# Seven-product pairs at every second place of the last product, and four buffers for each split part, in a two-layer hybrid trunk

## The chip, the core and the metric

The kernel runs on one core of a Trainium2 chip. Its time is the device time of one execution in microseconds (us); of several runs the median is taken. Five engines work side by side, each through its own queue in a fixed order: TensorE (PE) multiplies, VectorE (DVE) and ScalarE (ACT) do elementwise work, GpSimd (POOL) and SyncE (SP) mostly issue DMA transfers. They wait for each other by semaphores.

## The reference

One layer over 256 tokens of width 2048, all in float32:

```
h  = rmsnorm(x, norm1_g);  z = h @ w_in
a_out = forgetting_attention(...);  m_out = rmsnorm(mlstm(...)) * sigmoid(o)
merged = sigmoid(g_a) * (a_out @ w_proj_a) + sigmoid(g_m) * (m_out @ w_proj_m)
x  = x + merged @ w_out
h2 = rmsnorm(x, norm2_g)
u  = causal_dwconv(h2 @ w_up, conv_w, conv_b)          # 2 x 5632 channels, 3 taps
x  = x + (silu(u_gate) * u_val) @ w_down               # 5632 x 2048
```

The last line is the last product. It is the place where most of the change lies.

## The kernel before

**Two parts for each number.** TensorE multiplies in a short format (fp32r), so each float32 operand is split into a high part, which ScalarE rounds, and a low part, which VectorE makes as the difference between the operand and its high part. A product then takes three matmuls: low part of the activations by high weights, high by high, and high by low. The weights arrive as tiles `raw` of 128x2048 (three buffers, loaded on SP's queue, line 132). `split_sub` cuts each tile into pieces and makes `wh` on ScalarE (line 169) and `wl` on VectorE (line 170) for each piece, 128x1024 as a rule. There are three buffers of `wh` and three of `wl`, in turn. `next_sub(ahead)` hands the next piece to the matmuls and splits up to `ahead` pieces, that one included: two in most stages, three in `s_block`.

**Stages.** In order: the columns of `w_in` (`mog`, `fq`, `fk`, `fv`, `mk`, `mq`, `mv`), the gates (`g0` to `g3`), the two projections (`p`), the product with `w_out` (`wo0`, `wo1`), the product with `w_up` (`up`, 88 blocks), and the last product in two halves of 1024 columns, `y0` and `y1`.

**The last product.** 5632 rows of `w_down` make 44 blocks of 128, taken two at a time: 22 pairs for each half. A pair is done in one of two ways, by a string with one letter a pair (`Y_PAIRS`). A plain pair (`p`) has two pieces and eight products: 24 matmuls with 512 columns. A seven-product pair (`S`) is a Strassen-like scheme with seven products, 21 matmuls, in four pieces named `b` (two products), `b21` (one product, 128x512), `t13` and `t24` (two products each). `t13` and `t24` are sums and differences of the weights, which VectorE makes in a tile `sums`: line 154 from `b`'s tile (128x1024), then lines 161 and 164 (128x512 each). So an S costs VectorE three more operations than its low parts, and its last two pieces depend on them. The S products go into four accumulators `y0p`/`y1p`, the others into `y0q`/`y1q`; after the last S of a half a chain of one ScalarE copy and eight VectorE additions (lines 339 and 298) adds the `p` accumulators into `xr`, two of them behind each piece that follows; the half ends with four additions of `q` (line 974) and four stores.

**The ring.** The S pairs also need sums of the activations. They are made while `up` runs (`put_sums`), written to a tile in DRAM (`s_dram`, line 937) and read back by POOL's queue into ring tiles `s_ops`, each for two S pairs (line 952). One function, `load_sums`, is called twice ahead of the last product and then once whenever a new ring tile begins to be used, so that three tiles are in use or on their way.

**Where the order comes from.** The code is recorded as it is written, and a scheduler puts the instructions of each engine in a fixed order, as it finds them ready by its own reckoning; earlier-written work goes first. `issue_after(x)` forbids it to put an instruction ahead of `x`. Before the change the first operation on `sums` (line 154) is held behind the last write of the `up` stage alone, in the last product; nothing holds it in the earlier stages, so the scheduler may draw it forward among low parts.

**Large tiles.** Activations, gates, `sums` and ring tiles share one set of 15 buffers of 8 KB a partition (`a8`). While `up` runs, four of them hold its input `h2` and eleven the result (`ghl`).

Of the kernel before, what the change touches and what calls it, by code (L numbers as in the profile page):

```python
# [1 line left out]

# [1 line left out]

# [6 lines left out]
F32 = mybir.dt.float32  # L11
F32R = mybir.dt.float32r
# [5 lines left out]
P = 128  # L18
# [17 lines left out]
PLAIN = "p" * 8  # L36
G_PAIRS = "pSpSpSpp"
WO_PAIRS = "pSpSpppp"
Y_PAIRS = "ppp" + "SSpSp" * 3 + "Sp" + "pp"
N_S = Y_PAIRS.count("S")  # L40


# [18 lines left out]
def trunk(ctx: ExitStack, tc: tile.TileContext, a):  # L61
# [14 lines left out]
        return psaux.tile([P, 512], F32, tag="aux", name=name)  # L76

    def a8(name, shape, dtype=F32):
        return big.tile([P, *shape], dtype, tag="a8", bufs=15, name=name)

    def scratch(name, shape, tag="w2k", bufs=4):
        return work.tile(shape, F32, tag=tag, bufs=bufs, name=name)
# [51 lines left out]
    def split_sub(j):  # L134
        if j >= len(subs_of) or j in subs:
            return
        i, s, kind = subs_of[j]
        load_chunk(i)
        if j < KD:
            put(hT[j][:, 0, :], hT[j][:, 1, :], xT[j], cst[:, C_G1 + j : C_G1 + j + 1])  # L140
        n = 512 if kind == "b21" else chunks[i][1] // 2
        raw, sums = raws[i], s_tiles.get("sums")


        if kind == "whole":
            src = raw[:, s * n : (s + 1) * n]
        elif kind == "b":
            src = raw[:, 512:1536]
            if s_tiles["of"] != chunks[i][2]:
                s_tiles["of"] = chunks[i][2]  # L150
                s_tiles["sums"] = a8(f"sums{i}", [2048])
            sums = s_tiles["sums"]
            with tc.issue_after(last_of["up"].ins) if "up" in last_of else nullcontext():
                nc.vector.tensor_tensor(  # L154
                    sums[:, :1024].rearrange("p (i c) -> p i c", i=2),
                    raw[:, :512].unsqueeze(1).to_broadcast([P, 2, 512]),
                    src.rearrange("p (i c) -> p i c", i=2), ALU.subtract,
                )
        elif kind == "b21":
            src = raw[:, 1536:]  # L160
            nc.vector.tensor_tensor(sums[:, 1024:1536], raw[:, 1024:1536], sums[:, :512], ALU.subtract)
        elif kind == "t13":
            src = sums[:, :1024]
            nc.vector.tensor_tensor(sums[:, 1536:], raw[:, 1536:], sums[:, 1024:1536], ALU.subtract)
        else:
            src = sums[:, 1024:]
        wh = wpool.tile([P, 1024], F32R, tag="wh", bufs=3, name=f"wh{j}")
        wl = wpool.tile([P, 1024], F32R, tag="wl", bufs=3, name=f"wl{j}")
        nc.scalar.activation(wh[:, :n], src, AF.Copy)  # L169
        nc.vector.tensor_tensor(wl[:, :n], src, wh[:, :n].bitcast(F32), ALU.subtract)  # L170
        subs[j] = (wh[:, :n], wl[:, :n])

    state = {"sub": 0}
# [1 line left out]
    def next_sub(ahead=2):  # L175
        j = state["sub"]
        state["sub"] = j + 1
        i = subs_of[j][0]
        for c in range(i, i + 3):
            load_chunk(c)  # L180
        for q in range(j, j + ahead):
            split_sub(q)
        return subs.pop(j)
# [93 lines left out]
    def s_block(name, pairs, s_ops, pattern, pools, dst, add=True, per_piece=0):  # L277


        q = [[pools[0](f"{name}q{tok}{h}") for h in range(2)] for tok in range(2)]  # L280
        ps, late, left = {}, [], pattern.count("S")
        n_s = left

        def prod(out, x, w, c, first, last):
            wh, wl = w[0][:, c * 512 : (c + 1) * 512], w[1][:, c * 512 : (c + 1) * 512]
            mm(out, x[1], wh, first, False)
            mm(out, x[0], wh, False, False)
            mm(out, x[0], wl, False, last)

        def piece():  # L290
            w = next_sub(3)
            for _ in range(min(2, len(late))):
                late.pop(0)()
            run_tasks(per_piece)
            return w

        def tt(o, x, y):
            late.append(lambda: nc.vector.tensor_tensor(o, x, y, ALU.add))

        for m, kind in enumerate(pattern):  # L300
            def op(i, tok):
                t = slice(tok * P, (tok + 1) * P)
                return pairs[m][:, i, 0, t], pairs[m][:, i, 1, t]

            if kind == "p":
                last = m == len(pattern) - 1
                ws = [piece(), piece()] if last else []

                todo = (
                    [(i, tok, h) for h in range(2) for tok in range(2) for i in range(2)] if last  # L310
                    else [(i, tok, h) for i in range(2) for h in range(2) for tok in range(2)]
                )
                for i, tok, h in todo:
                    if i == len(ws):
                        ws.append(piece())
                    prod(q[tok][h], op(i, tok), ws[i], 1 - h, m == 0 and i == 0, last and i == 1)
                continue
            first, last = left == n_s, left == 1
            left -= 1
            s1, s2, s3, s4 = s_ops[m]  # L320
            w = piece()
            if first:
                ps = {i: pools[1](f"{name}p{i}") for i in (1, 5, 7, 6)}
            prod(ps[1], op(0, 0), w, 0, first, last)
            prod(q[0][1], s4, w, 1, False, False)
            prod(q[0][0], op(1, 0), piece(), 0, False, False)
            w = piece()
            prod(ps[5], s1, w, 0, first, last)
            prod(ps[7], s3, w, 1, first, last)
            w = piece()  # L330
            prod(ps[6], s2, w, 0, first, last)
            prod(q[1][0], op(1, 1), w, 1, False, False)
            if not last:
                continue
            c11, c12, c21, c22 = (dst(tok, h) for tok in range(2) for h in range(2))
            u2 = scratch("u2", [P, 512])
            if add:
                u3 = scratch("u3", [P, 512])
                late.append(lambda: nc.scalar.activation(u2, ps[1], AF.Copy))
                tt(c11, c11, ps[1])  # L340
                tt(u2, u2, ps[6])
                tt(u3, u2, ps[7])
                tt(u2, u2, ps[5])
                tt(c21, c21, u3)
                tt(u3, u3, ps[5])
                tt(c12, c12, u2)
                tt(c22, c22, u3)
            else:
                late.append(lambda: nc.scalar.activation(c11, ps[1], AF.Copy))
                tt(u2, c11, ps[6])  # L350
                tt(c21, u2, ps[7])
                tt(c12, u2, ps[5])
                tt(c22, c21, ps[5])
        for f in late:
            f()
        return q
# [564 lines left out]
    for j in range(NF):  # L921
# [12 lines left out]
        if Y_PAIRS[m] == "S":  # L934
# [3 lines left out]
                s_dram[:, n_s * 6 * P : (n_s + 1) * 6 * P], se.rearrange("p l c -> p (l c)")  # L938
            )
            n_s += 1  # L940
        last_of["up"] = put_pair(g_pairs[m], gv)


    s_pos = [m for m, kind in enumerate(Y_PAIRS) if kind == "S"]
# [13 lines left out]
        at = [ring[r][:, q * P : (q + 1) * P] for q in range(6 * i, 6 * i + 6)]  # L958
        return [(g[:, 0, 0, P:], g[:, 0, 1, P:])] + [(at[c], at[3 + c]) for c in range(3)]

    for _ in range(2):
        load_sums()
    for b in range(2):
        pools = (acc_tile, aux_tile) if b == 0 else (aux_tile, acc_tile)
        xr = big.tile([P, 2, 1024], F32, tag="mv", name=f"xr{b}")
# [86 lines left out]
```

## Time and profile before

| | |
|---|---|
| median of 3 runs | 1402.15 us (1394.18 to 1404.11) |
| the profiled execution | 1393.67 us, span 1391.9 us |
| PE busy | 1375.6 us, 99% |
| DVE busy | 1070.9 us, 77% |
| ACT busy | 767.2 us, 55% |
| `up` begins / last product begins / its second half begins | 661.9 / 1150.7 / 1269.8 us |
| TensorE clock granted | 1.00 in all stages |
| weight tile of `w_down`, issue to landing | 4.9 us median |
| ring tile, issue to landing | 4.7 us median, 4.4 to 10.6 |

The span goes from the first to the last instruction of the profiled execution; its own time is 1.8 us longer than the span. Start times are counted from the span's start. A matmul with 512 columns is shown as 0.39 us long, but the next one starts about 0.227 us after it, since matmuls are pipelined: time lost on PE is seen as a longer step between starts, and only the larger part of it as idle time.

### The profile page before, as it was taken

The numbers are of one execution on the slowest core, as the hardware profiler recorded it, in microseconds if no ns is written. First come the engines' busy times: TensorE is split into PE (matmuls) and PEld (weight loads), VectorE is DVE, ScalarE is ACT, GpSimd is POOL, SyncE is SP. The second block draws the span as 40 slices with busy tenths as digits, with TensorE's granted clock in tenths as the row PEclk, the third lists the DMA queues.
The fourth block names the chain that finished last, engine by engine and source line by source line (L and its number), as shares of the span: only waits on it lengthen the run. The fifth ranks groups of instructions, "written<-read, shape, count | busy, mean of one in ns | idle before, by whom it ended". The sixth has DMA issues, their size and how long they took to land.

```text
span 1391.9 us, 18433 instructions
## 1 busy us (share of the span) xinstructions
PE 1375.6 (99%) x6940; PEld 1157.2 (83%) x6940; DVE 1070.9 (77%) x1524; ACT 767.2 (55%) x1096; POOL 40.4 (3%) x73
## 2 busy tenths in 40 slices
PE   9999999999999999999999999999999999999998
PEld 8878888887888888888888888888888887778776
DVE  5655766556888867777878888888878888887987
ACT  6645554444665544555655555555655655553553
POOL 2101000000000000000000000000000000000000
PEclk9999999999999999999999999999999999999999
DMA  8645454443554565555555655655555657668553
GB/s 312 229 165 184 179 209 155 152 151 134 196 215 182 214 241 194 190 220 203 191 186 194 218 193 190 222 186 196 201 212 194 230 196 266 226 251 291 205 209 119
DMA packets 44073, 281.76 MB, mean 202 GB/s; under 512 B 5008, under 2 KB 5024, under 8 KB 13264
## 3 DMA queue, kind: packets, MB, share of 16 engines
q1 hardware_dynamic: 39168, 260.20, 52.4%
q0 software_dynamic: 4672, 20.38, 4.2%
q8 instruction: 54, 0.88, 0.2%
q14 instruction: 35, 0.29, 0.1%
q10 hardware_dynamic: 144, 0.02, 0.0%
HBM read 272.45 MB, written 8.13 MB: 202 GB/s over the span
## 4 chain that ended last, share of the span: by engine, by line
PE 96%; DVE 1%; issue 1%; ACT 1%; DMA 1%; POOL 0%; DVEq 0%; ACTq 0%; POOLq 0%
PE up L230 35%; PE p L230 6%; PE y1q L230 6%; PE y0q L230 5%; PE mog L230 3%; PE fq L230 3%; PE mv L230 3%; PE fk L230 3%; PE fv L230 3%; PE wo0q L230 3%; PE wo1q L230 3%; PE g1q L230 2%; PE g3q L230 2%; PE g2q L230 2%; PE g0q L230 2%; PE y1p L230 2%
## 5 line engine op out<-in xcount | busy, mean ns | idle before, releaser
L169 ACT ACTIVATE wh<-raw 128x1024 fp32r<-128x1024 f32 (+2 forms) x496 | 502.7, 1017 | 473.9 <-PE up L230 117.9
L170 DVE TENSOR_TENSOR wl<-raw,wh 128x1024 fp32r<-128x1024 f32 (+2 forms) x496 | 575.1, 1169 | 205.3 <-ACT wh L169 203.5
L230 PE MATMUL up<-h,wh 128*128 128x512 f32 x1408 | 488.6, 394 | 0.0
L230 PE MATMUL up<-h,wl 128*128 128x256 f32 x1408 | 390.0, 277 | 0.0
L230 PEld LDWEIGHTS up<-h,wh 128*128 128x128 f32 x1408 | 263.9, 188 | 61.4 <-DVE h L199 0.2
L230 PEld LDWEIGHTS up<-h,wl 128*128 128x128 f32 x1408 | 264.4, 188 | 0.1
L170 DVE TENSOR_TENSOR wl<-sums,wh 128x1024 fp32r<-128x1024 f32 x66 | 80.6, 1222 | 43.9 <-ACT wh L169 43.5
L169 ACT ACTIVATE wh<-sums 128x1024 fp32r<-128x1024 f32 x66 | 69.9, 1060 | 78.6 <-PE y0q L230 16.6
L909 DVE SCALAR_TENSOR_TENSOR t<-u,cst,t 128x256 f32<-128x256 f32 x176 | 84.7, 481 | 3.8 <-ACT t L907 0.7
L230 PE MATMUL p<-wh,am 128*128 128x512 f32 x256 | 79.6, 392 | 0.0
L230 PE MATMUL y1q<-wh,ghl 128*128 128x512 f32 x232 | 71.7, 390 | 0.0
L230 PE MATMUL y0q<-wh,ghl 128*128 128x512 f32 x232 | 71.7, 390 | 0.0
L230 PEld LDWEIGHTS p<-wh,am 128*128 128x128 f32 x256 | 47.6, 188 | 9.7
L907 ACT ACTIVATE t<-u,cst 128x256 f32<-128x256 f32 x88 | 52.0, 591 | 2.4 <-DVE u L904 1.9
L230 PEld LDWEIGHTS y1q<-wh,ghl 128*128 128x128 f32 x232 | 43.6, 188 | 9.2
L230 PEld LDWEIGHTS y0q<-wh,ghl 128*128 128x128 f32 x232 | 43.5, 188 | 9.1
L230 PE MATMUL p<-wl,am 128*128 128x512 f32 x128 | 49.9, 390 | 0.0
L230 PE MATMUL y1q<-wl,ghl 128*128 128x512 f32 x116 | 44.8, 391 | 0.0
L230 PE MATMUL y0q<-wl,ghl 128*128 128x512 f32 x116 | 44.8, 390 | 0.0
L154 DVE TENSOR_TENSOR sums<-raw 128x1024 f32<-128x1024 f32 x33 | 40.4, 1223 | 4.7 <-DMA raw<-in_w_dn 3.0
L230 PE MATMUL mog<-wh,hT 128*128 128x348 f32 (+1 forms) x192 | 42.4, 331 | 1.3 <-ACT wh L169 1.3
L230 PE MATMUL g0q<-wh,hN 128*128 128x512 f32 x128 | 41.3, 401 | 0.0
(370 smaller groups left out, 2064.0 us busy)
## 6 DMA issues: line engine op xcount, KB each, us to landing
raw<-in_w_up SPq DMA_DIRECT2D x88, 1024.0 KB, 4.9
raw<-in_w_dn SPq DMA_DIRECT2D x44, 1024.0 KB, 4.9
raw<-in_w_g SPq DMA_DIRECT2D x32, 1024.0 KB, 4.9
raw<-in_w_fox SPq DMA_DIRECT2D x24, 1024.0 KB, 4.9
raw<-in_w_p SPq DMA_DIRECT2D x16, 1024.0 KB, 4.8
raw<-in_w_out SPq DMA_DIRECT2D x16, 1024.0 KB, 4.8
raw<-in_w_mqk SPq DMA_DIRECT2D x8, 1024.0 KB, 4.8
raw<-in_w_mv SPq DMA_DIRECT2D x8, 1024.0 KB, 4.8
```

The source lines that it names most:

```text
L154: nc.vector.tensor_tensor(sums[:, :1024].rearrange("p (i c) -> p i c", i=2), raw[:, :512].unsqueeze(1).to_broadcast([P, 2, 512]), src.rear ...
L169: nc.scalar.activation(wh[:, :n], src, AF.Copy)
L170: nc.vector.tensor_tensor(wl[:, :n], src, wh[:, :n].bitcast(F32), ALU.subtract)
L230: nc.tensor.matmul(out, lhsT, rhs, start=start, stop=stop)
L907: nc.scalar.activation(t, u[:, 2:], AF.Identity, scale=w[2], bias=w[3])
L909: nc.vector.scalar_tensor_tensor(out=t, in0=u[:, i : i + S], scalar=w[i], in1=t, op0=ALU.mult, op1=ALU.add)
```

## The change

`Y_PAIRS` goes from `pppSSpSpSSpSpSSpSpSppp` to `pSpSpSpSpSpSpSpSpSpSpp`: ten S pairs as before, but never two in a row, with the first at place 1 in the place of 3 and the last at place 19 in the place of 18. In `s_block` four pieces are split ahead in the place of three, and there are four buffers each of `wh` and `wl`. These two hold for the gates and `w_out` too, which use the same function. The memory for them comes from the large tiles: 14 in the place of 15. The ring is two tiles: `load_sums` is called once ahead, not twice. The first operation on `sums` is now held, in all stages, behind the low part that was recorded last.

```diff
-Y_PAIRS = "ppp" + "SSpSp" * 3 + "Sp" + "pp"
+Y_PAIRS = "p" + "Sp" * 10 + "p"
...
-        return big.tile([P, *shape], dtype, tag="a8", bufs=15, name=name)
+        return big.tile([P, *shape], dtype, tag="a8", bufs=14, name=name)
...
-            with tc.issue_after(last_of["up"].ins) if "up" in last_of else nullcontext():
+
+            with tc.issue_after(last_of["wl"].ins):
                 nc.vector.tensor_tensor(
                     sums[:, :1024].rearrange("p (i c) -> p i c", i=2),
...
-        wh = wpool.tile([P, 1024], F32R, tag="wh", bufs=3, name=f"wh{j}")
-        wl = wpool.tile([P, 1024], F32R, tag="wl", bufs=3, name=f"wl{j}")
+        wh = wpool.tile([P, 1024], F32R, tag="wh", bufs=4, name=f"wh{j}")
+        wl = wpool.tile([P, 1024], F32R, tag="wl", bufs=4, name=f"wl{j}")
         nc.scalar.activation(wh[:, :n], src, AF.Copy)
-        nc.vector.tensor_tensor(wl[:, :n], src, wh[:, :n].bitcast(F32), ALU.subtract)
+        last_of["wl"] = nc.vector.tensor_tensor(
+            wl[:, :n], src, wh[:, :n].bitcast(F32), ALU.subtract
+        )
...
         def piece():
-            w = next_sub(3)
+            w = next_sub(4)
...
-        last_of["up"] = put_pair(g_pairs[m], gv)
+        put_pair(g_pairs[m], gv)
...
-    for _ in range(2):
-        load_sums()
+    load_sums()
```

VectorE's order in `y0`, before, from the last plain piece ahead of the first two S pairs (places 3 and 4, weight tiles 207 and 208). Pieces are numbered through the kernel: 440 to 443 are the first S, 444 to 447 the second.

```order
L154 TENSOR_TENSOR sums207_10411<-raw207_10375 128x1024
L170 TENSOR_TENSOR wl439_10394<-raw206_10337,wh439_10393 128x1024
L161 TENSOR_TENSOR sums207_10411<-raw207_10375,sums207_10411 128x512
L164 TENSOR_TENSOR sums207_10411<-raw207_10375,sums207_10411 128x512
L170 TENSOR_TENSOR wl440_10414<-raw207_10375,wh440_10413 128x1024
L170 TENSOR_TENSOR wl441_10431<-raw207_10375,wh441_10430 128x512
L170 TENSOR_TENSOR wl442_10452<-sums207_10411,wh442_10451 128x1024
L154 TENSOR_TENSOR sums207_10411<-raw208_10409 128x1024
L170 TENSOR_TENSOR wl443_10466<-sums207_10411,wh443_10465 128x1024
L170 TENSOR_TENSOR wl444_10474<-raw208_10409,wh444_10473 128x1024
L161 TENSOR_TENSOR sums207_10411<-raw208_10409,sums207_10411 128x512
L170 TENSOR_TENSOR wl445_10485<-raw208_10409,wh445_10484 128x512
```

The same engine at place 3 after the change, from the two plain pieces ahead (tile 206) to the first plain piece behind (tile 208); the `sums` tile is now named after tile 205, and all lines are three or one higher.

```order
L171 TENSOR_TENSOR wl440_10400<-raw206_10335,wh440_10399 128x1024
L171 TENSOR_TENSOR wl441_10407<-raw206_10335,wh441_10406 128x1024
L155 TENSOR_TENSOR sums205_10341<-raw207_10383 128x1024
L171 TENSOR_TENSOR wl442_10418<-raw207_10383,wh442_10417 128x1024
L162 TENSOR_TENSOR sums205_10341<-raw207_10383,sums205_10341 128x512
L171 TENSOR_TENSOR wl443_10431<-raw207_10383,wh443_10430 128x512
L165 TENSOR_TENSOR sums205_10341<-raw207_10383,sums205_10341 128x512
L171 TENSOR_TENSOR wl444_10448<-sums205_10341,wh444_10447 128x1024
L171 TENSOR_TENSOR wl445_10466<-sums205_10341,wh445_10465 128x1024
L171 TENSOR_TENSOR wl446_10476<-raw208_10427,wh446_10475 128x1024
```

An S takes seven VectorE operations in both; what moved is its neighbour (a plain pair, not the next S), and its first sum, which stands directly behind the low part of the piece ahead.

VectorE's order near the end of `y0` before, at the S pairs at places 16 and 18 (tiles 220 and 222), with the plain pair of tile 221 between them.

```order
L170 TENSOR_TENSOR wl484_10970<-sums207_10411,wh484_10969 128x1024
L154 TENSOR_TENSOR sums207_10411<-raw222_10966 128x1024
L170 TENSOR_TENSOR wl485_10980<-sums207_10411,wh485_10979 128x1024
L170 TENSOR_TENSOR wl486_10987<-raw221_10928,wh486_10986 128x1024
L170 TENSOR_TENSOR wl487_10997<-raw221_10928,wh487_10996 128x1024
L170 TENSOR_TENSOR wl488_11010<-raw222_10966,wh488_11009 128x1024
```

And after, at place 17 (tile 221), behind the plain pair of tile 220:

```order
L171 TENSOR_TENSOR wl481_10928<-sums205_10341,wh481_10927 128x1024
L171 TENSOR_TENSOR wl482_10938<-raw220_10889,wh482_10937 128x1024
L171 TENSOR_TENSOR wl483_10945<-raw220_10889,wh483_10944 128x1024
L155 TENSOR_TENSOR sums205_10341<-raw221_10925 128x1024
L171 TENSOR_TENSOR wl484_10956<-raw221_10925,wh484_10955 128x1024
```

Before, a sum that needs a new weight tile stands ahead of three low parts that don't; after, all that stands behind it until the next plain pair needs the same tile.

POOL's queue from the first load of the last product on, before:

```order
L952 DMA s_ops0_10327<-s_dram_5501 128x1536
L952 DMA s_ops1_10329<-s_dram_5501 128x1536
L952 DMA s_ops2_10446<-s_dram_5501 128x1536
L952 DMA s_ops3_10570<-s_dram_5501 128x1536
L952 DMA s_ops4_10690<-s_dram_5501 128x1536
L952 DMA s_ops5_10844<-s_dram_5501 128x1536
L952 DMA s_ops6_10964<-s_dram_5501 128x1536
L952 DMA s_ops7_11313<-s_dram_5501 128x1536
L967 DMA xr1_11203<-xs_4785 128x2x1024
```

And after:

```order
L955 DMA s_ops0_10327<-s_dram_5505 128x1536
L955 DMA s_ops1_10381<-s_dram_5505 128x1536
L955 DMA s_ops2_10539<-s_dram_5505 128x1536
L955 DMA s_ops3_10693<-s_dram_5505 128x1536
L955 DMA s_ops4_10847<-s_dram_5505 128x1536
L955 DMA s_ops5_11001<-s_dram_5505 128x1536
L955 DMA s_ops6_11248<-s_dram_5505 128x1536
L969 DMA xr1_11206<-xs_4785 128x2x1024
L955 DMA s_ops7_11406<-s_dram_5505 128x1536
```

The loads keep their order but for `xr1`, the residual of the second half, which now stands ahead of ring tile 7. Two waits of them are different. Ring tile 0 waits for the matmuls of the last `up` block on the second quarter of `h2` (before: the first quarter), because the last tile of `ghl`, the fifteenth large tile, now takes the first quarter's buffer, and its first write on ScalarE waits for that. Ring tile 2 waits until both S pairs of ring tile 0 are done (before: it took the buffer of the fourth quarter of `h2`).

On PE the 21 matmuls of an S now stand piece by piece as they are written; before, those of an S pair that followed another were interleaved with their neighbours.

More of the change, by code (lines that the diff above doesn't have):

```diff
@@ L1 @@
-from contextlib import ExitStack, nullcontext
+from contextlib import ExitStack
 import numpy as np
```

## The prediction

> **What bounds the kernel now.** The head of the page and its line of busy time come first.
>
> ```profile
> span 1391.9 us, 18433 instructions
> PE 1375.6 (99%) x6940; PEld 1157.2 (83%) x6940; DVE 1070.9 (77%) x1524; ACT 767.2 (55%) x1096; POOL 40.4 (3%) x73
> ```
>
> PE sets the time, and the number of matmuls does not change. So the change can win only the time in which PE stands still or is spaced out. Next, the waits of PE, which say for whom it stood still (total, times, longest):
>
> ```profile
> PE y1p L230 <- ACT wh L169: 2.4, 3, 0.8
> PE y0p L230 <- ACT wh L169: 2.4, 3, 0.8
> PE ps_mt L778 <- DVE mo L766: 1.8, 1, 1.8
> PE y0p L230 <- DVE wl L170: 1.5, 1, 1.5
> ...
> PE wo1p L230 <- DVE wl L170: 0.3, 1, 0.3
> ```
>
> Nearly all is in the last product: three stops in each half for a high part, and one for a low part. The chain of waits (start, length, count) gives the spacing without stops:
>
> ```profile
> 673.87 477.02 PE up L230 x2752
> 1150.88 16.35 PE y0q L230 x72
> 1370.50 16.84 PE y1q L230 x74
> ```
>
> `up` has no step to win: it runs as one row. In the last product 72 matmuls take 16.35 us, 0.2271 each. A half has 12 plain pairs of 24 and 10 S pairs of 21, 498 matmuls; two halves 996, at 0.2271 us 226.2 us. They took from 1150.88 to 1370.50 + 16.84 = 1387.34, 236.5 us. **The last product loses 10.3 us**, and that is the purse of this change. The timeline of PE shows the shape of a stop (start, length):
>
> ```profile
> 1174.48 0.63 PE L230 MATMUL y0p<-wh,s_ops 128*128 128x512 f32 x2
> 1175.92 0.51 PE L230 MATMUL y0p<-wh,s_ops 128*128 128x512 f32 x1 [0.81 <-ACT wh L169]
> 1176.26 0.40 PE L230 MATMUL y0p<-wl,ghl 128*128 128x512 f32 x1
> ...
> 1240.44 1.07 PE L230 MATMUL y0q<-wh,ghl 128*128 128x512 f32 x4
> 1242.96 0.50 PE L230 MATMUL y0p<-wl,s_ops 128*128 128x512 f32 x1 [1.46 <-DVE wl L170]
> 1243.30 0.40 PE L230 MATMUL y0q<-wl,ghl 128*128 128x512 f32 x1
> ```
>
> The first: 1175.92 - 1174.48 - 2 x 0.227 = 0.99, and 0.11 more to the next start: 1.10 us. It is the second S of a pair of neighbours; three such neighbours a half, and three waits a half in the rows above, so 6 x 1.10 = 6.6 us. The second: 2.52 - 4 x 0.227 = 1.61, and 0.11: 1.7 us, once. Together 8.3 of the 10.3; the other 2.0 is small spacing, mostly around the sums.
>
> Why it stops stands in VectorE's timeline, from the second S's first sum on:
>
> ```profile
> 1169.39 1.23 DVE L154 TENSOR_TENSOR sums<-raw 128x1024 f32<-128x1024 f32 x1
> 1170.54 1.22 DVE L170 TENSOR_TENSOR wl<-sums,wh 128x1024 fp32r<-128x1024 f32 x1
> 1171.67 1.22 DVE L170 TENSOR_TENSOR wl<-raw,wh 128x1024 fp32r<-128x1024 f32 x1
> 1172.81 0.68 DVE L161 TENSOR_TENSOR sums<-raw,sums 128x512 f32<-128x512 f32 x1
> 1173.41 0.68 DVE L170 TENSOR_TENSOR wl<-raw,wh 128x512 fp32r<-128x512 f32 x1
> 1174.01 0.68 DVE L164 TENSOR_TENSOR sums<-raw,sums 128x512 f32<-128x512 f32 x1
> 1174.61 2.51 DVE L170 TENSOR_TENSOR wl<-sums,wh 128x1024 fp32r<-128x1024 f32 x2
> 1177.04 2.35 DVE L170 TENSOR_TENSOR wl<-raw,wh 128x1024 fp32r<-128x1024 f32 x2
> 1179.31 1.22 DVE L154 TENSOR_TENSOR sums<-raw 128x1024 f32<-128x1024 f32 x1
> ```
>
> It runs without a gap. By steps between starts an S costs 1.15 (sum) + 1.14 + 0.60 + 0.60 + 0.60 + 2.43 = 6.5 us, a plain pair 2.3 us. PE needs 21 x 0.2271 = 4.8 us for an S and 5.45 for a plain pair. Two S in a row ask VectorE for 13.0 us in 9.5 of PE. ScalarE's row shows the consequence:
>
> ```profile
> 1174.81 1.06 ACT L169 ACTIVATE wh<-sums 128x1024 fp32r<-128x1024 f32 x1 [1.90 <-DVE sums L164]
> ```
>
> `t24`'s high part waits for the last sum, and PE for it. The second kind of stop is an order and not a load:
>
> ```profile
> 1232.65 7.81 DMA raw<-in_w_dn
> 1240.55 1.23 DVE L154 TENSOR_TENSOR sums<-raw 128x1024 f32<-128x1024 f32 x1 [1.66 <-DMA raw<-in_w_dn]
> ```
>
> The sum for place 18 stands ahead of the low part that PE needs for place 16, and its weight tile is still in flight.
>
> **The change, part by part.**
>
> *S pairs at every second place.* An S and a plain pair ask VectorE for 6.5 + 2.3 = 8.8 us in 4.8 + 5.45 = 10.2 of PE: 1.4 us of slack in each period, where two neighbours overran by 3.5. The six stops of 1.10 go: -6.6.
>
> *Four buffers, four pieces ahead.* The tightest part of an S is `t24`. With four buffers it takes the buffer of the second plain piece, free when the S begins; 1.06 (ScalarE) + 1.22 (VectorE) later, at 2.3 us, it is ready, and PE wants it after 15 matmuls, at 3.4 (its low part two matmuls later). So 1.1 us is left. With three buffers it had to wait for `b`'s six matmuls (1.36) and was ready at 3.6 at best. The first plain piece behind has 4.8 - 1.4 = 3.4 us for the same 2.3. No stop should take the place of those removed; what is late next is this `t24`, by a margin of 1.1.
>
> *Sums behind the low parts in front.* Now all that stands behind a sum waiting for its weight tile needs the same tile, up to the next plain pair. A tile's load can be issued when the plain pair three places ahead has its low parts, one period of 10.2 us before; 7.81 fits. The 1.7 us stop goes. What it costs: a sum is never drawn forward, which matters only if VectorE is late at a plain pair, against 1.4 us of slack.
>
> *Two ring tiles.* A later ring tile is loaded when both S pairs of the one before last are done, and wanted five pairs later (S or plain, some 26 us); no landing comes near that. The start is tight. These are POOL's first loads and the landing times of all ten; the last row is that of the second load alone:
>
> ```profile
> 1148.41 0.53 POOL L952 DMA_DIRECT2D s_ops<-s_dram  x1 [0.83 <-PE up L230]
> 1151.18 0.53 POOL L952 DMA_DIRECT2D s_ops<-s_dram  x1 [2.24 <-PE up L230]
> ...
> DMA to landing us min/median/max: 4.4/4.7/10.6
> s_ops<-s_dram POOLq DMA_DIRECT2D x1, 768.0 KB, 7.0
> ```
>
> Ring tile 0 now waits for the second quarter of `h2`, as tile 1 does here, so 1148.41. The first S is at place 1: PE wants the sums after 24 + 3 matmuls, at 1150.88 + 27 x 0.2271 = 1157.0. From the nearest row, 7.0 us, it lands at 1155.4, 1.6 us in time; from the slowest, 10.6, at 1159.0, a stop of 2.0 us. I take none, since tile 1's load here met two others and tile 0's will meet no more, and keep 2.0 for the range. The Trainium skill, in "DMA: Bandwidth & Descriptors", section on queues, rings and completion order, says that each DMA engine goes round-robin over its queues packet by packet, so a ring tile and a weight tile in flight slow each other; with the fixed 2.0 us and 436 GB/s of its section on the anatomy of one DMA, both (1.84 MB) land in an estimated 6.2 us, which gives no stop either. The trace's 7.0 is longer than the estimate.
>
> The skill has a rule that speaks against feeding PE so from POOL's queue: "SBUF — State Buffer", in the section on who interferes with whom, lets a VectorE operation with two inputs in SBUF block GpSimd's reads until it ends. If that held up the ring's issue, one operation of 1.22 us would leave 0.4 of the 1.6. The two issues above take 0.53 us each, with VectorE at 85% of the stage (below), so the trace shows no such block.
>
> *One buffer less for large tiles.* Only the last tile of `ghl` lacks one: its high part on ScalarE waits for the last `up` block's first quarter. Behind it stands the high part of place 1's first piece, whose own buffer is freed by the same block's first half, later still; wanted at 1150.88 + 5.45 = 1156.3. Cost 0, cover over 5 us. PE needs that `ghl` tile at places 20 and 21, 100 us on.
>
> *The last S one place later.* Its nine closing operations now have four pieces in front of the end, not six, so one is left for behind the half. Eight VectorE additions of 0.68 are 5.4 us:
>
> ```profile
> L298 DVE TENSOR_TENSOR u<-u,y0p x4: 677/678/687, 1255.9 to 1261.3; 128x512 f32<-128x512 f32 x4
> ...
> 1150.70:1269.80 119.10, 115.24 (x501) 91.82 (x500) 101.80 (x112) 63.56 (x69) 3.19 (x6) 1.00 0.68 246
> 1269.80:1387.40 117.60, 115.11 (x499) 91.48 (x497) 99.41 (x106) 60.28 (x64) 1.79 (x3) 1.00 0.56 201
> ```
>
> Behind the last S PE has two plain pairs, 10.9 us, against 5.4 + 4 low parts (4.6) on VectorE: it fits in the second half, so the end of the kernel stays. In the first half the next pairs' low parts come on top, but `y1` wants the last of these accumulators only 2.0 us into its first pair; 0, with 0.7 (one addition) as the bound. (The two rows are busy time by stage: span, PE, PEld, DVE, ACT, POOL.) VectorE's 101.8 of 119.1 is the 85%, and the change adds no operation.
>
> *Small spacing and the other stages.* Of the 2.0 us I take half, -1.0; the ends are 0 and -2.0. In `wo1p` 0.3 may go. At `ps_mt` VectorE's low parts move by one place against the operation waited for: -1.8 to +1.2 (one low part); I take 0, as what it waits for is a chain of small operations through three engines.
>
> **The sum.** -6.6 - 1.7 - 1.0 = -9.3: span 1382.6, and with the 1.8 us outside it 1384.4 against the profiled 1393.67. The runs shown reach from 1394.18 to 1404.11, their median 8.5 above the profiled one; the same drop from the median is 1402.15 - 9.3 = **1392.9 us**. About 1% (14 us) is what a measurement of this kernel can tell from no change.
>
> **The rivals.**
>
> *Every S stops.* If `t24`'s margin of 1.1 is not there (handing over between PE, ScalarE, VectorE and back takes more than counted, or sums held back behind low parts come late), each S pays the stop that only neighbours pay now: 20 x 1.10 = 22.0 for 8.3, span 1391.9 + 13.7 = 1405.6, median 1415.9. It decides as soon as a period costs VectorE more than 10.2 us. For it: the waits of `wh` on sums, as in ScalarE's row. Against: the S at places 6, 11 and 18 stand alone even now, with three buffers, and PE's waits name only three stops a half for a high part. 0.08.
>
> *The gain goes elsewhere.* The stops move to the start of `y0` (2.0), to the change of halves (0.7) or to the gates and `w_out`, where the sums are held back for the first time; at a third to all of the gain lost, 1396 to 1402. For it: landings up to 10.6. Against: margins of 1.1 us and more at each place. 0.14.
>
> *More than forecast.* All 10.3, `ps_mt`'s 1.8 and some at the start of the kernel, -13: 1389. 0.10.
>
> The forecast itself has 0.68.
>
> **Chances.** The three runs shown lie 9.9 us apart, so the median may fall to either side: with the low ones the forecast would be 1384.9, with the high one 1394.8. I give the forecast case 0.2 of being faster by over 1% (below 1388.1), the larger gain 0.6, and slower by over 1% half of the case that every S stops. Faster 0.2 x 0.68 + 0.6 x 0.10 + 0.04 for a low draw of the third case = 0.24; slower 0.04, rounded up to 0.05 for the unnamed; within 1% 0.71. The range goes from 1383 (the low runs and the forecast, or more) to 1403 (no gain in the median).
>
> **What would show it.** Right: no wait of `y0p` or `y1p` for `wh` over 0.2 us; VectorE idle some 1 us in each period; the stage 227 to 228 us long; sums following their weight tile without a low part waiting behind. Wrong: a stop at PE's first `s_ops` matmul near 1157 (ring), stops at each `t24` (buffers), or as much idle time on PE in other stages as left this one.

## The result, and the profile after

| | median of 6 | lowest to highest | profiled run | span |
|---|---|---|---|---|
| before | 1404.01 us | 1394.18 to 1405.35 | 1393.67 us | 1391.9 us |
| after | 1379.13 us | 1378.91 to 1379.15 | 1379.12 us | 1377.3 us |

The ratio is 0.9834, with a 95% interval of 0.9808 to 0.9861: faster by 1.7%. The forecast was 1392.9 us, in a range from 1383 to 1403: it was 13.8 us too high, and the measured time lies 4 us below the low end of the range. Two questions come out of the table. The span fell by 14.6 us where 9.3 were forecast, and the median fell by 24.9, 10.3 more than the span.

The head of the page of after, and its line of busy time:

```profile
span 1377.3 us, 18383 instructions
PE 1368.3 (99%) x6940; PEld 1162.5 (84%) x6940; DVE 1070.4 (78%) x1524; ACT 766.9 (56%) x1096; POOL 40.1 (3%) x73
```

All waits of PE that are left (total, times, longest):

```profile
PE ps_mt L781 <- DVE mo L769: 1.8, 1, 1.8
PE mog L233 <- ACT wh L170: 1.2, 1, 1.2
PE ps_warm L389 <- DVE first L391: 1.2, 1, 1.2
PE mog L233 <- DVE wl L171: 0.4, 1, 0.4
```

No `y0` or `y1` row is among them. The chain of waits (start, length, count) shows the last product as an even beat, a stretch of 27 plain matmuls and then the S part, for the whole of its length:

```profile
670.01 477.02 PE up L233 x2752
1147.02 5.47 PE y0q L233 x24
1152.49 0.68 PE y0p L233 x3
1153.17 1.36 PE y0q L233 x6
1154.53 2.04 PE y0p L233 x9
1156.57 6.12 PE y0q L233 x27
...
1361.25 11.57 PE y1q L233 x51
```

It ends at 1372.82: 225.8 us, which is the whole of 996 matmuls at 0.2267. Busy time by half of the last product (span, PE, PEld, DVE, ACT, POOL) says the same, PE without a gap and VectorE at 100.71 of 112.91, so 12.2 us idle over ten periods:

```profile
1147.02:1259.93 112.91, 112.91 (x500) 93.47 (x499) 100.71 (x111) 64.11 (x69) 3.18 (x6) 1.00 0.70 253
1259.93:1372.85 112.92, 112.88 (x498) 93.12 (x497) 97.78 (x107) 59.57 (x63) 2.31 (x4) 1.00 0.59 216
```

Where the span went, by the first matmul of each product in PE's timeline (the last product to the end of its last matmul):

| stretch | before | after | difference |
|---|---|---|---|
| start of `mog` | 6.54 | 6.42 | -0.12 |
| `mog` | 49.71 | 48.45 | -1.26 |
| `fq` to the end of `g0` | 299.83 | 299.86 | 0.03 |
| `g1`, `g2`, `g3` | 125.69 | 124.44 | -1.25 |
| `p` | 90.01 | 90.01 | 0 |
| `wo0`, `wo1` | 86.44 | 85.29 | -1.15 |
| `ps_h` and `up` | 492.50 | 492.39 | -0.11 |
| last product | 236.62 | 225.95 | -10.67 |

The sum is -14.5. So 10.7 us are the last product's and 3.9 come from products in which the forecast had none.

### The profile page after: what moved, and what is told of

It is laid out like the page before. It is cut to its first block, busy times and chain, and to the rows that moved or that the text cites. A ratio compares the mean times of both kernels' runs of the same rounds, so it can differ in the third digit from the quotient of the medians.

```text
span 1377.3 us, 18383 instructions
## 1 busy us (share of the span) xinstructions
PE 1368.3 (99%) x6940; PEld 1162.5 (84%) x6940; DVE 1070.4 (78%) x1524; ACT 766.9 (56%) x1096; POOL 40.1 (3%) x73
## 4 chain that ended last, share of the span: by engine, by line
PE 98%; DVE 1%; ACT 0%; DMA 0%; issue 0%; POOL 0%; SPq 0%; DVEq 0%; ACTq 0%
PE up L233 35%; PE p L233 6%; PE y0q L233 6%; PE y1q L233 6%; PE mog L233 3%; PE fq L233 3%; PE mv L233 3%; PE fk L233 3%; PE fv L233 3%; PE wo0q L233 3%; PE wo1q L233 3%; PE g0q L233 3%; PE g3q L233 2%; PE g2q L233 2%; PE g1q L233 2%; PE y1p L233 2%
## 5 line engine op out<-in xcount | busy, mean ns | idle before, releaser
L233 PE MATMUL p<-wl,am 128*128 128x512 f32 x128 | 49.9, 390 | 0.0
L233 PE MATMUL mv<-wh,hT 128*128 128x512 f32 x128 | 40.2, 395 | 0.0
```

The source lines that it names most:

```text
L233: nc.tensor.matmul(out, lhsT, rhs, start=start, stop=stop)
```

## Experiments

### The kernel before once more: two paces of the up blocks

`e0` is the kernel before, without an edit.

> The kernel before, unchanged, to see whether its spread from 1394 to 1405 us is in the span itself. Theory A (the kernel's own stops vary from run to run, through sums that wait for a weight tile in front of low parts): the spans differ by up to 10 us with the granted clock at 1.00 in all, and a profile of a long run has further stops of PE for low parts or high parts in the last product, where the profile of before had 8.3 us of them. Theory B (the runs differ outside the span or by the clock): spans within 1 us of 1391.9, or longer only where the clock is lower.

Measured: 12 runs, 1392.7 and eleven from 1401.61 to 1405.75. The profiled one is a long one, span 1400.7, granted clock 1.00. Its last product takes 236.5 as before, with the same six stops for high parts and stops for low parts at other places. What is 9.2 us longer is one row of the chain of waits; the first row is of the profile of before, the second of this one:

```profile
673.87 477.02 PE up L230 x2752
```

```profile
673.61 486.19 PE up L230 x2752
```

The row is unbroken in both: PE waits for nothing in it. 2752 matmuls are 1376 couples (a high part against 512 columns, a low part against 256): 346.7 ns a couple in the one, 353.3 in the other. In the groups of the profile's page, the mean of one matmul goes from 394 and 277 ns to 399 and 281. The other stages keep their lengths to 0.35 us (`mog` 0.34 longer, the gates 0.26 shorter); from the first matmul of `fq` to the first of `g0` it is 241.98 and 241.99. So theory A is right that the span itself differs, and wrong on the place, and theory B is wrong: the difference is in the span, at the same clock, as a **pace of the up blocks that differs from run to run of one program**. The Trainium skill, in "TensorE: Matmul & The Clock Gate", section on the back-to-back issue gap, says that in a stream of weight loads and matmuls the spacing is set by both operations together. No run here shows which of the two makes the two paces.

### An interruption can switch the pace

`e7` is before, and `f3` is after, with the same addition:

```
     for j in range(NF):
+        if j in (8, 16, 24, 32):
+            pause = acc_tile(f"pause{j}")
+            for tok in range(2):
+                nc.tensor.matmul(pause[:, tok * P : (tok + 1) * P], ident, ones, start=True, stop=True)
```

> The kernel before with four added interruptions of PE among the up blocks (two matmuls of 128 columns on constants into an unused accumulator, ahead of blocks 8, 16, 24 and 32; some 0.5 us each, 2 us in all). If the pace of the up blocks (347 or 353 ns a couple) is drawn anew after each interruption: the profile shows stretches of both, and times lie between 1395 and 1407 in more than two groups. If it belongs to the run: one pace throughout the 470 us, two groups of times 9 us apart.

> The changed kernel with the four interruptions of PE among the up blocks (two matmuls of 128 columns on constants ahead of blocks 8, 16, 24 and 32, some 0.5 us each). If an interruption draws the pace anew in this kernel too: times in several groups between 1381 and 1388, a profile with stretches of both. If the changed kernel holds the quick pace by itself: all within 1 us of 1381.

Measured: `e7` 1399.38 median of 12, eight spread from 1395.23 to 1401.06 and four from 1405.22 to 1406.55; `f3` 1388.2 median of 6, two at 1381.8 and 1382.3, four from 1387.9 to 1388.6. The chain of waits of `e7`, then of `f3`:

```profile
674.97 79.14 PE up L230 x448
754.56 88.75 PE up L230 x512
843.76 88.75 PE up L230 x512
...
1022.16 133.13 PE up L230 x768
```

```profile
669.36 77.66 PE up L233 x448
747.47 90.45 PE up L233 x512
838.36 90.45 PE up L233 x512
...
1020.15 135.68 PE up L233 x768
```

In `e7` the first 224 couples run at 353.3 ns and all behind the first interruption at 346.7; in `f3` it is the other way round, 346.7 and then 353.3. So the first case of both expectations came, stretches of both paces in one run. Both switches stand exactly at an interruption, one in each direction, and between interruptions the pace holds. Not every interruption switches it: three of four left it as it was in both profiles.

### Pairs of parts: what each of the three is worth

The change has three parts: the order of the pairs, the queue (sums behind the low parts in front), the depth (four buffers, four pieces ahead). Two of three at a time, from after:

```
e1, order and queue:  -bufs=4 +bufs=3 (wh, wl);  -next_sub(4) +next_sub(3)
e2, order and depth:  -with tc.issue_after(last_of["wl"].ins):
                      +with tc.issue_after(last_of["up"].ins) if "up" in last_of else nullcontext():
                      (and last_of["up"] is set again)
e3, queue and depth:  -Y_PAIRS = "p" + "Sp" * 10 + "p"
                      +Y_PAIRS = "ppp" + "SSpSp" * 3 + "Sp" + "pp"
```

> The changed kernel with three buffers for each part and three pieces ahead again; order, queued sums and two ring tiles stay. Order theory (the prediction's: the order of the pairs takes the stops away, buffers only widen margins): the last product 226 to 231 us (t24 ready at 3.6 us where PE wants it at 3.4, so at most 0.2 for each of 20), the first product's 1.3 us come back, span 1378.6 to 1383. Depth theory (the fourth buffer takes the stops away): every S pair stops by about 1.1, 22 us in the last product, span about 1400.

> The changed kernel with its sums held back as before (free in the gates and the output projection, behind the last of the up blocks in the last product), so that they may be drawn forward. If the queue took the stop at the low part away and the 2.4 us that the gates and the output projection gained: the stop of 1.7 in the last product is back once or more, gates and output projection lose 2.4, span 1379.7 to 1382, and the times spread again by up to 10 us (theory A). If four pieces ahead did it: span 1377 to 1378, times within 0.5 us of each other.

> The changed kernel with the old order of the pairs (three times two seven-product pairs side by side in each half); four buffers, queued sums and two ring tiles stay. Order theory: six stops of 1.1 us are back, last product 232 to 234, span 1384 to 1386. Depth theory (one more piece of lead, 1.4 us of PE or more, covers a stop of 1.1): no stop, span 1377 to 1379.

And one at a time, from before: `e4` has only the new `Y_PAIRS`, `e5` only `issue_after(last_of["wl"].ins)`, `e6` only the four buffers, `next_sub(4)` and, to make room, `bufs=14` and one `load_sums()` ahead.

> The kernel before with the new order of the pairs alone; three buffers, three pieces ahead, sums held as before. Order theory of the prediction: the six stops of 1.1 go, the last product takes 229 to 230 us, span 1385. Joint theory (a sum drawn forward waits for a weight tile in front of low parts, and more places are open to that when every second pair has sums; order with depth but without the queue took 241.8): last product 238 to 250, span 1394 to 1405 at the quick pace of the up blocks. Pace: at three buffers most runs at 353 ns a couple of up matmuls, some 9 us longer than the shortest.

> The kernel before with the sums queued behind the low parts alone; old order, three buffers. If the queue is what works: gates and output projection gain 1 to 2.4 us, the stop of 1.7 is gone, and the six stops of 1.1 stay (last product 232 to 235) or go too, if it was the early sums and not the load of two neighbours that made them (227 to 230). If only depth works: last product 236 as before. Pace: at three buffers half or more of the runs 9 us above the shortest.

> The kernel before with four buffers for each part, four pieces ahead and the smaller ring alone; old order, old hold of the sums. If depth is what works: the six stops go, last product 228 to 231. If the early sums are the cause, depth without the queue leaves stops for low parts: last product 234 to 242. Pace of the up blocks: if the fourth buffer brings the quick one, at least 10 of 12 runs lie in the lower cluster, and up takes 492.5 us; if it is a draw of the run, as many long ones as in before.

Lengths from the profiles, in us; the ratio to before is of the timed runs. Depth, and queue with depth, stand with both of their profiles (`e6` and `g0`, `e3` and `g1`).

| parts | last product | `g1` to `g3` | `wo` | `mog` | ratio (95%) |
|---|---|---|---|---|---|
| none (before) | 236.6 | 125.7 | 86.4 | 49.7 | |
| order | 245.9 | 126.0 | 86.6 | 49.9 | 1.0071 (1.0058 to 1.0084) |
| queue | 235.4 | 125.6 | 85.8 | 50.1 | 0.997 (0.9955 to 0.9985) |
| depth | 229.0, 228.1 | 124.4 | 85.3 | 48.6 | 0.9913 (0.99 to 0.9926), 0.99 (0.9861 to 0.994) |
| order, queue | 227.5 | 125.4 | 85.9 | 50.4 | 0.9896 (0.9866 to 0.9927) |
| order, depth | 241.8 | 125.1 | 85.3 | 48.6 | 0.9965 (0.9939 to 0.999) |
| queue, depth | 228.9, 228.8 | 124.4 | 85.3 | 48.7 | 0.9849 (0.9826 to 0.9872), 0.9874 (0.9842 to 0.9905) |
| all (after) | 225.9 | 124.4 | 85.3 | 48.5 | 0.9834 (0.9808 to 0.9861) |

(The ratios mix the two paces of `up`; the lengths don't.) Four readings:

**Order alone costs 9.2 us**, and order with depth 5.2. The first and the last row of the last product of `e4` in the chain of waits, and PE's waits in it:

```profile
1160.51 2.51 PE y0q L230 x11
...
1394.83 11.37 PE y1q L230 x50
```

```profile
PE y0p L230 <- DVE wl L170: 6.5, 4, 1.7
PE y1p L230 <- DVE wl L170: 3.1, 2, 2.9
PE y0p L230 <- ACT wh L169: 1.9, 1, 1.9
```

The six stops for high parts of neighbours are gone, and one of 1.9 near the start has come; but stops for low parts have taken their place, 9.6 us where before had 1.5. Some 3 us more came from the clock: about 1 us behind the stops of 1.9 and 2.9 the granted clock was 0.50 for 3.4 us each, in which matmuls step at 0.427 us in the place of 0.227. The order theory had 229 to 230 for this kernel and was 16 us off; the joint theory, 238 to 250, was right. For order with depth a loss of 1.7 or little more was expected, a span of 1382 at most; it was 1393.9, with these stops:

```profile
PE y1p L233 <- DVE wl L171: 4.0, 3, 2.9
PE y0p L233 <- DVE wl L171: 3.5, 3, 1.7
```

The longest stop of order alone in the timeline of VectorE and in the chain of waits:

```profile
1307.56 1.23 DVE L154 TENSOR_TENSOR sums<-raw 128x1024 f32<-128x1024 f32 x1 [3.14 <-DMA raw<-in_w_dn]
1308.70 1.22 DVE L170 TENSOR_TENSOR wl<-sums,wh 128x1024 fp32r<-128x1024 f32 x1
```

```profile
1298.75 8.71 DMA raw<-in_w_dn
...
1308.70 1.23 DVE wl L170
...
1309.97 0.50 PE y1p L230
```

VectorE stands 3.1 us at a sum whose weight tile has 8.7 us on its way, and behind it stands the low part that PE wants at once. It is the stop that the prediction found once in before, at more places.

**With the queue, no such stop is left**: `e5` has no wait of the last product for a low part, and its six stops for high parts are all there:

```profile
PE y1p L232 <- ACT wh L169: 2.4, 3, 0.8
PE y0p L232 <- ACT wh L169: 2.4, 3, 0.8
```

**Behind the queue, order takes the six stops away with three buffers** (235.4 to 227.5), and **with four buffers they go without order and without queue as well**. Depth alone, at 229.0 and 228.1, has no stop of the last product for a high part; one for a low part is left, of 2.3 in `e6` and 1.4 in `g0`, again behind a sum whose tile is on its way:

```profile
PE y1p L230 <- DVE wl L170: 2.3, 1, 2.3
```

So the fourth buffer by itself brings 7.6 to 8.5 of the 10.7. The queue then takes that stop away (longest wait 0.2), but gains nothing in sum, 228.9 and 228.8, since at the neighbours 18 steps of PE are now 0.11 to 0.13 too long (one of them, at the wait, 0.3). The order is worth the last 3.0, most of it these steps. So of the two theories of the expectations neither holds alone: the depth theory's 22 us of stops with three buffers did not come, and neither did the order theory's six stops with four.

**Depth gives the gain outside the last product**, in every kernel that has it: 1.2 to 1.3 us in `g1` to `g3` against the profile of before (1.0 against that of `e0`; 0.6 in `e2`, which has one late low part), 1.1 in `wo`, and `mog` at 47.9 to 48.8 over all profiles with four buffers, where three give 49.7 to 51.0. The queue alone gives 0.1 and 0.6 and nothing in `mog`.

### Four buffers or four pieces ahead

`g3` is after with `next_sub(3)`, four buffers kept.

> The changed kernel with four buffers but parts made three pieces ahead in the last product, the gates and the output projection (the fourth buffer then gives ScalarE a free buffer a piece earlier, but PE's lead is three pieces). If the gain of depth there (gates 1.25, output projection 1.1, last product 1.6 against three buffers) is the lead: it is lost, span 1381. If it is that ScalarE no longer waits for a buffer: it stays, span 1377 to 1378, and the first product keeps its 1.3 to 2 in both cases, since its lead is two pieces throughout.

Measured: profile 1377.3 us of span; `mog`, the gates, `wo` and the last product as in after to 0.01 us; 1379.17 median. So the fourth piece of lead gives nothing. `e1` and `g3` differ only in the number of buffers: from three to four the last product goes from 227.5 to 225.9, the gates from 125.4 to 124.4, `wo` from 85.9 to 85.3 and `mog` from 50.4 to 48.5. So it is the fourth buffer that gives the gain. What it does to the times of the parts is to be seen at an S pair of `g3q`, in ScalarE's and VectorE's timeline of before and then of after:

```profile
446.74 1.06 ACT L169 ACTIVATE wh<-sums 128x1024 fp32r<-128x1024 f32 x1 [0.30 <-PE g3q L230]
447.73 1.23 DVE L154 TENSOR_TENSOR sums<-raw 128x1024 f32<-128x1024 f32 x1
448.88 1.22 DVE L170 TENSOR_TENSOR wl<-sums,wh 128x1024 fp32r<-128x1024 f32 x1
```

```profile
443.15 1.06 ACT L170 ACTIVATE wh<-sums 128x1024 fp32r<-128x1024 f32 x1 [1.64 <-PE g3q L233]
444.25 1.23 DVE L171 TENSOR_TENSOR wl<-sums,wh 128x1024 fp32r<-128x1024 f32 x1 [1.48 <-ACT wh L170]
```

The S pair begins at 445.57 in before (443.29 in after). With three buffers `t24`'s high part waits for PE to release the buffer of a piece of the same S and is ready 2.2 us into it; a sum of the next S slips in, and the low part is ready at 450.10, 4.5 us in; by the count of the prediction PE would want it at 3.9. PE's queue has that low part four matmuls later here, at 450.19, so that its step is only 0.07 too long. With four buffers the low part is ready at 445.48, 2.2 us in. The 1.2 us of the gates lie in seven steps that are 0.07 to 0.23 too long, 0.7 in all, and in many of 0.23 to 0.24 in the place of 0.227; what makes each of them too long is not shown.

### Which programs run at the quick pace

`f0` and `g2` are after once more, `g0` and `g1` are `e6` and `e3` once more, and `f1` and `f2` are after and before with

```
-    for _ in range(9):
+    for _ in range(10):
         nc.tensor.matmul(ps_warm, warm[:, :P], warm, start=True, stop=True)
```

> The changed kernel, unchanged, beside more runs of the one before. If the quick pace of the up blocks (347 ns a couple, 9 us less than at 353) belongs to the changed program, all runs lie within 1 us of 1379. If it was the luck of six runs or of one chip, some lie near 1388, as 53 of 58 runs of before lie above 1401.

> The changed kernel with ten warming matmuls on zeros in place of nine at its start, while PE waits for its first weights anyway: no cost of its own expected (0 to 0.3 us), every later instruction of PE one place on. If the pace hangs on the wait pattern that the change made, it stays quick: 1379. If it hangs on where in the program the instructions lie, runs near 1388 turn up.

> The kernel before with ten warming matmuls in place of nine: no cost expected. If the pace hangs on the place of the instructions, the share of long runs (above 1401) moves, to few or none; if on the wait pattern, most stay above 1401.

> Four buffers, four ahead and the smaller ring alone, once more, beside the changed kernel on one chip. If this part brings the quick pace of the up blocks and the first runs (all five long) fell to a chip on which everything ran long: most runs near 1381 to 1383 (the lower group, 9 us below the 1391 of the first time). If it does not: all near 1391 again.

> Four buffers and queued sums in the old order, once more, beside the changed kernel on the same chip. If queue and depth together bring the quick pace: as the first time, all or nearly all at 1382. If it is the chip: the same share of long runs as the changed kernel and the four buffers alone have beside it.

> The changed kernel a third time, beside its parts on one chip: so far 11 of 12 runs at 1379 and one at 1388. If the pace is the program's, again at most one or two long ones; if it is the chip's, as many as the two kernels beside it.

Measured, over all comparisons (each set of kernels ran on another chip; one run of before, at 7875 us, is left out):

| program | runs at the quick pace | quick | long |
|---|---|---|---|
| before, all its runs | 12 of 91 | median 1394.5 | median 1403.7 |
| before, ten warming matmuls | 2 of 12 | 1393.3, 1394.1 | 1401.7 to 1406.0 |
| queue | 2 of 12 | 1391.7, 1392.0 | 1401.0 to 1401.5 |
| order, queue | 3 of 6 | 1383.9 to 1384.1 | 1393.0 to 1393.1 |
| depth (`e6`, `g0`) | 0 of 5, 4 of 6 | 1381.3 to 1384.6 | 1390.4 to 1392.7 |
| queue, depth (`e3`, `g1`) | 11 of 11 | 1381.7 to 1382.6 | |
| after, all its runs | 17 of 19 | 1378.4 to 1379.3 | 1388.0, 1388.2 |
| after, ten warming matmuls | 5 of 5 | 1378.4 to 1379.5 | |
| after, three pieces ahead | 5 of 6 | 1378.7 to 1379.2 | 1388.1 |

With order alone and with order and depth the stops themselves vary from run to run by several us, so the groups can't be told by the time; the profile of the one has the long pace, that of the other the quick one. The profile of `g2` caught one of the two long runs of after:

```profile
669.84 486.18 PE up L233 x2752
```

Beside `mog`, which varies by some 0.8 us, and its start, which varies by 0.3, it is the only stretch that differs from the other profiles of after by more than 0.2. So the quick pace isn't sure in the changed program, only frequent. One warming matmul more at the start of PE's program moves the share in neither kernel, which speaks against the place of the instructions as the cause. The runs of depth alone that were all long the first time were not the program's nature: beside after on another chip four of six were quick. Which part brings it stays open: with queue and fourth buffer together it was there in 38 of 41 runs (the last four rows), with neither in 14 of 103, with one alone in between; but the set counts too: before had no quick run among 22 in the set in which depth had none of 5, and 5 of 11 in the set in which depth had 4 of 6. No wait of PE tells the two paces apart. In both profiles of before, quick and long, the last break in PE's work ahead of the long row is the same step behind `ps_rb`, 0.42 us to the next start where 0.23 is usual.

## Why the prediction was wrong, and where it was right

**The step that failed for the median is the last one of the sum**, "the same drop from the median". It took the 8.5 us between the profiled run of before and the median as something that both kernels would have. It is the long pace of `up`, 9.2 us, which 79 of 91 runs of before have and 2 of 19 of after. At the same pace the change is worth 1394.5 - 1379.1 = 15.4 us between the quick runs and 1403.7 - 1388.1 = 15.6 between the long ones; the other 9 of the measured 24.9 are the pace. Of the 13.8 us that the forecast was off, 8.5 are this step and 5.3 the span, 3.9 of them in the other stages and 1.4 in the last product's small spacing. Why the changed program has the quick pace so much more often is not known. The profile of before could not show it, since that was a run of the quick pace; but three runs of 1402, 1394 and 1404 against 1393.67 in the profile did say that the profiled run was not the usual one, and that what made up the 8.5 us was not in it.

**The six stops, -6.6: the size was right, the cause only half.** They are gone. But the order by itself takes them away at a loss: alone it makes the product 9.2 us longer. The sentence that two neighbours ask for 13.0 us of VectorE in 9.5 of PE holds with three buffers and queued sums (235.4 to 227.5). The prediction added the three edits up; the runs show that they act together, and that the queue is what the order needs. It did not say that with the fourth buffer alone the six stops would go too, neighbours or not: it gave the buffer a margin only.

**The one stop, -1.7: right**, and so is its cause; the queue alone takes it away. In before it is not always one: the long profile has two there, of 0.7 at most.

**Small spacing, -1.0: mis-sized**, the choice of half between 0 and -2.0. All of it went, so that the last product became 10.7 shorter, its whole purse and, since the even beat runs at 0.2267 and not at 0.2271, a little more.

**Other stages, 0: the step that failed for the span.** They gave 3.9: `mog` 1.3 (and its start 0.1), `g1` to `g3` 1.25, `wo` 1.15. The prediction's term for them was nothing, though the gates and the output projection have 13 S pairs (nine and four) that use the same buffers. It had worked out that with three buffers `t24` is ready at 3.6 us at best where PE wants it at 3.4, and used that for the last product alone. At 0.2 each the 13 pairs would make 2.6, and 2.4 were measured, but that is luck: 3.6 is the time of the low part, which by the same count PE wants at 3.9, and the trace has other steps (above); in `wo` one stop with its two long steps makes 0.6 alone. `wo1p`'s 0.3 was all it saw, since the view of waits lists what stops PE, and these spacings are too short to be waits. `mog` has no S pair; ScalarE's waits for PE to release a buffer fall there from 6.4 to 3.7 us; how this shortens the product was not followed further. `ps_mt` kept its 1.8, as taken.

**The margins held.** `t24` in the last product of after, on ScalarE and VectorE, for the S pair from 1162.69:

```profile
1162.55 1.06 ACT L170 ACTIVATE wh<-sums 128x1024 fp32r<-128x1024 f32 x1 [1.66 <-PE y0q L233]
1163.64 1.23 DVE L171 TENSOR_TENSOR wl<-sums,wh 128x1024 fp32r<-128x1024 f32 x1 [0.88 <-ACT wh L170]
```

It is ready at 1164.87, 2.2 us in (2.3 forecast), 1.2 ahead of PE. The first ring tile, POOL's issue and the answer on that load alone:

```profile
1144.55 0.56 POOL L955 DMA_DIRECT2D s_ops<-s_dram  x1 [26.17 <-PE up L233]
```

```profile
DMA to landing us min/median/max: 7.5/7.5/7.5
```

It landed at 1152.05 and was wanted at 1153.17, 1.1 in time where 1.6 were forecast. The estimate of 6.2 from the Trainium skill's "DMA: Bandwidth & Descriptors", section on the anatomy of one DMA, was short by 1.3. The closing operations, the last `ghl` tile and the change of halves cost nothing. The issues of ring tiles in `y0` took 0.53 each with VectorE at 89%. The rule of the Trainium skill's "SBUF — State Buffer", section on who interferes with whom, is about GpSimd's reads of SBUF, and the trace shows no effect of it on these issues.

**The rivals.** That every S stops, and that the gain goes elsewhere, were both wrong, though without the queue the product does get slower than before (order and depth: 241.8), with stops at some of the S pairs and for another reason, sums that wait for their tile. (Of the S pairs that stood alone in before, the prediction left out the one at place 16; nothing hangs on it.) "More than forecast" was nearest on the span, -13 for -14.6, with the right two sources of three. It had no term for the gates and the output projection, and its 1389 rested on the same median. The signs named in advance came out right: no wait in `y0p` and `y1p`, some 1.2 us of idle VectorE in each period, no idle time added in other stages; only the stage was 225.8 long, below its 227 to 228.

## What to carry to other kernels

An instruction that waits for a DMA, placed ahead of ready work in an engine's queue, can cost more than the imbalance one is trying to mend: mend the queue first, since an order that is better on paper may lose without it. A deeper buffer acts on every stage that uses it, so its effect is to be looked for in all of them, also below what a view of waits lists. Where the timed runs lie in two groups, find out which group the profiled run is of and what makes the other before subtracting anything from a median.

## What was not expected of the hardware

One program of matmuls, with no wait in it and at a granted clock of 1.00, ran at 346.7 or at 353.3 ns for a couple of 512 and 256 columns, for 470 us on end, 9.2 us in all; an interruption of PE by two small matmuls could switch it, in both directions (`e7`, `f3`). The stages from `fq` to `g0`, mostly of matmuls with 512 columns, did not show it; nor did the 128 couples of 512 and 256 columns in `mq` and `mk` among them, whose median step from start to start is 350.0 ns in all 18 profiles. What sets the pace isn't known from these runs.

At two stops of PE in `e4` (1.9 and 2.9 us) and at one in `e2` (2.9) the granted clock fell to 0.50 for 3.4 us, from 0.3 us before to 1.2 us behind the stop's end; behind the stop of 2.3 in `e6` it stayed at 1.00. What decides this isn't shown.
